# Memory keys and values at plain float32 from the loaded weights, the norm weights in the memory

## Chip, cores and metric

The kernel runs on one core of one Trainium2 chip. The metric is the device time of one execution in microseconds (us), here the median of three runs. All data are float32. The kernel hands float32 data to TensorE under two types, `F32R` (less precise) and plain `F32`.

## The reference, cut to what matters

Two layers of an encoder on 256 tokens of width 1024. The even layer mixes by RWKV-7 and a state-space model (S5), the odd one by differential attention; either is followed by cross-attention to a memory of 256 rows, then by a feed-forward part (dense in the first layer, the two best of eight experts in the second). What the change touches is the left side of the cross-attention, which depends on the memory alone:

```python
def rms_norm(x, gain):
    y = x * rsqrt(mean(x * x, axis=-1) + 1e-6)
    return y * gain

def memory_cross_attention(h, mem_n, w_q, w_kv, q_gain, k_gain, w_o):
    q = rms_norm((h @ w_q).reshape(b, t, 4, 256), q_gain)
    k, v = split(mem_n @ w_kv, 2)            # w_kv: 1024 x 2048
    k = rms_norm(k.reshape(b, m, 4, 256), k_gain)
    p = softmax(q . k * 256 ** -0.5)
    return (p @ v) @ w_o

# in layer l: mem_n = rms_norm(mem, norm_mem[l])
```

The factor of a memory row, the rsqrt, is the same in both layers; the norm weights `norm_mem[l]` and the weights `w_kv[l]` are a layer's own.

## The kernel before, in words

Every large product is made to a higher precision than one `F32R` matmul gives. A float32 operand is split in two: ScalarE writes its high half as `F32R` (`AF.Copy`), VectorE subtracts that from the operand and writes the low half. `mm3` (line 188) then adds three `F32R` matmuls to one PSUM tile: high by high, high by low, low by high (lines 190, 191, 192). `mm` (line 194, its matmul in line 195) issues one matmul of whatever type its operands have; with `F32` operands it is a plain float32 one, which the trace shows as two records. The split weights of the large products come from `chunks` (line 164), which loads, splits and yields them.

The first third of a millisecond holds the RWKV and S5 mixing of the first layer. It is a chain of small products and elementwise work that goes back and forth between TensorE, VectorE, ScalarE and GpSimd. The keys and values of both layers, which depend on the memory alone, are computed beside it as filler:

- `memory_norm` (line 462) loads the memory in two blocks of 128 rows, multiplies each by its rsqrt factor, and has `transpose_split` (line 203) transpose it, four pieces of 128 columns to a PSUM tile, and write it split, as `mth` and `mtl` (128 x 8 x 256 each).
- `fchunks` (line 437) loads the weights of 512 output columns, two blocks of 128 rows at a time, into `fraw` (pool `frw`, two buffers) from SP's queue. Each block is split: ScalarE multiplies it by the norm weights of its rows and writes the high half `fwh` (line 450), VectorE does the same product, subtracts and writes the low half `fwl` (line 453). Pool `fwp` has three buffers of each.
- `memory_kv` (line 477) does this for the two layers: for each of four groups of 512 output columns and each of eight blocks of rows it issues two `mm3`, one per block of memory rows, into the two PSUM tiles `pf`; then it scales, transposes and stores keys, or copies and stores values. That makes 2 x 4 x 8 x 2 = 128 memory products.

`memory_kv` is a generator: after every product it yields an estimate of TensorE's time in us, `0.65`. `pipeline` (in the kernel's first part) deals out such steps. It walks through the steps of the chain with estimated costs and waits, and puts steps of the filler between them: the memory products, then the rest of the S5 scan, the S5 gate (`s5_gate`) and the first half of the out projection (`hy_first`). The filler gets half a us per us of the chain (`FILL_B`), 16 us ahead of it (`FILL_C`), and every estimated wait. The order in which the code is issued in this way is a priority; in this part of the kernel the framework's scheduler makes each engine's own order from it, and from there every engine runs its queue in order. Norm and first filler steps are issued with a lowered priority (`LPM`, `LPF`).

After this part the kernel frees its pools, and the second half of the out projection, the first cross-attention, the dense feed-forward part, the second layer's attention and the experts follow. The order of TensorE is written out by hand there. The keys and values come back from DRAM for either cross-attention.

Of the kernel before, what the change touches and what calls it, by code (L numbers as in the profile page):

```python
# [8 lines left out]
F32 = mybir.dt.float32  # L9
F32R = mybir.dt.float32r  # L10
I32 = mybir.dt.int32
AF = mybir.ActivationFunctionType
# [111 lines left out]
def kernel(ctx: ExitStack, tc: tile.TileContext, a: dict, out: bass.AP, dbg=None):  # L124
# [10 lines left out]
    def scoped(cx, name, bufs, **kw):  # L135
        return cx.enter_context(tc.tile_pool(name=name, bufs=bufs, reuse_waits="tile", **kw))
# [87 lines left out]
    xtp1 = pool("xtp1", 1, reuse_waits="tile", side="right")  # L224
    cright = ExitStack()
    fkp = scoped(cright, "fkp", 1, side="right")
    frw = scoped(cright, "frw", 2, side="right")
    fwp = scoped(cright, "fwp", 3, side="right")
    fs2 = scoped(cright, "fs2", 2, side="right")
    smf = scoped(cright, "smf", 2, side="right")  # L230
    cx = ExitStack()
# [202 lines left out]

    low_priority(lambda: [behind(S5BT, lambda: s5_table(m)) for m in range(2)], LPT)

    def fchunks(src, nk=8, gain=None):
        for r in range(0, nk, 2):
            raw = frw.tile([128, 1024], F32, name="fraw", tag="fraw")
            nc.sync.dma_start(raw, src[:, r * 512:(r + 2) * 512])  # L440
            for j in range(2):
                wh = fwp.tile([128, 512], F32R, name="fwh", tag="fwh")
                wl = fwp.tile([128, 512], F32R, name="fwl", tag="fwl")
                rv = raw[:, j * 512:(j + 1) * 512]
                if gain is None:
                    nc.scalar.activation(wh, rv, AF.Copy)
                    nc.vector.tensor_tensor(wl, rv, wh, op=ALU.subtract)
                else:
                    g = col(gain, r + j)
                    nc.scalar.activation(wh, rv, AF.Copy, scale=g)  # L450
                    e_ = nc.gpsimd if FG[W["fg"] % len(FG)] == "g" else nc.vector
                    W["fg"] += 1
                    e_.scalar_tensor_tensor(wl, rv, g, wh, op0=ALU.mult, op1=ALU.subtract)  # L453
                yield r + j, wh, wl


    kdr = [tc.dram_tile([4, 128, 512], F32, name=f"kdr{l}") for l in range(2)]
    vdr = [tc.dram_tile([4, 128, 512], F32, name=f"vdr{l}") for l in range(2)]
    mth = fkp.tile([128, 8, T], F32R, name="mth")
    mtl = fkp.tile([128, 8, T], F32R, name="mtl")  # L460

    def memory_norm():
        for b in range(2):
            mem = sp.tile([128, D], F32, name="mem", tag="mem")
            nc.sync.dma_start(mem, a["mem"][b * 128:(b + 1) * 128, :])
            ss = smf.tile([128, 1], F32, name="ss", tag="ss")
            for i in range(2):
                kx = fs2.tile([128, 512], F32, name="kx", tag="kx")
                s1 = ss if i == 0 else smf.tile([128, 1], F32, name="ssb", tag="ssb")
                nc.scalar.activation(kx, mem[:, i * 512:(i + 1) * 512], AF.Square, accum_out=s1)  # L470
            nc.gpsimd.tensor_tensor(ss, ss, s1, op=ALU.add)
            rs = smf.tile([128, 1], F32, name="rs", tag="rs")
            rsqrt_small(rs, ss, 1, 1.0 / D, EPS, smf)
            nc.vector.tensor_scalar(mem, mem, rs, None, op0=ALU.mult)
            transpose_split(mem, mth, mtl, 0, b, ps_fl, "fl")

    def memory_kv(l):
        gg = const.tile([128, 2], F32, name=f"gg{l}")
# [2 lines left out]
        nc.gpsimd.tensor_tensor(gg, cols[:, lo:hi], cols[:, lo2:hi2], op=ALU.mult)  # L481
        for n in range(4):
            p = [ps_fl.tile([128, 512], F32, name="pf", tag="fl") for b in range(2)]
            for k, wh, wl in fchunks(a["wkv"][4 * l + n], 8, f"gm{l}"):
                for b in range(2):
                    t = slice(b * 128, (b + 1) * 128)
                    mm3(p[b], (mth[:, k, t], mtl[:, k, t]), (wh, wl), k == 0, k == 7)
                    yield 0.65
            for b in range(2):
                kx = fs2.tile([128, 512], F32, name="kx", tag="kx")  # L490
                if n >= 2:
# [1716 lines left out]
```

## Time and profile before

| what | us |
|---|---|
| median of three runs | 1673.35 |
| lowest and highest run | 1672.85, 1676.12 |
| the profiled execution | 1672.61 |
| its span, first to last instruction | 1670.8 |
| TensorE busy | 1619.4 (97%) |
| VectorE busy | 639.9 (38%) |
| ScalarE busy | 476.1 (28%) |
| GpSimd busy | 198.5 (12%) |

The shares are means over parts of the run that have different limits, so the rows below are given by stretch. In the profile PE is TensorE's matmuls and PEld its weight loads, DVE is VectorE, ACT ScalarE, POOL GpSimd and SP the engine that issues most DMAs. Matmuls overlap, and their ends are modelled: a TensorE that is busy all the time may still have room. How fast matmuls follow one another is read from their starts in the timeline. In the chain of waits every piece is work that was waited for, or the instruction before it on the same engine; "issue" is time in which nothing that the profile shows was waited for.

### The profile page before, as it was taken

How to read it: one execution, taken by the hardware profiler on the slowest of the kernel's cores; microseconds unless marked ns; L12 is line 12 of the kernel's file. 1: busy time of each engine (PE TensorE's matmuls, PEld its weight loads, DVE VectorE, ACT ScalarE, POOL GpSimd, SP SyncE). 2: the span in 40 equal slices, each digit the busy share in tenths (PEclk: the TensorE clock that was granted, in tenths of full speed). 3: DMA queues.
4: the chain of work that ended last, by engine and by line, in shares of the span. 5: the costliest groups of instructions: out<-in, count | busy, mean ns of one | idle time of the engine just before them, and what ended most of it. 6: DMA issues, size and time to landing. Idle time of an engine off the chain costs nothing.

```text
span 1670.8 us, 34308 instructions
## 1 busy us (share of the span) xinstructions
PE 1619.4 (97%) x14882; PEld 982.9 (59%) x14882; DVE 639.9 (38%) x1065; ACT 476.1 (28%) x852; POOL 198.5 (12%) x230
## 2 busy tenths in 40 slices
PE   6999999999999999999999999999999999999997
PEld 5877657899999988998334333343333433333432
DVE  7778987676555567764100011100101001010011
ACT  6466434555544456653101000010000100010000
POOL 6334473111000031110000000000000000000000
PEclk9999979999999999998999999999999999999999
DMA  6423323664555543646699889999999999999995
GB/s 227 152 89 127 109 71 115 222 255 152 186 193 180 195 156 116 239 150 239 252 387 383 333 356 407 415 418 419 419 418 418 419 419 419 418 419 387 372 419 218
DMA packets 74462, 471.48 MB, mean 282 GB/s; under 512 B 8600, under 2 KB 10008, under 8 KB 22464
## 3 DMA queue, kind: packets, MB, share of 16 engines
q1 hardware_dynamic: 73024, 465.02, 71.5%
q0 software_dynamic: 1280, 4.20, 0.7%
q8 instruction: 118, 1.93, 0.5%
q14 instruction: 40, 0.33, 0.1%
HBM read 463.94 MB, written 5.24 MB: 281 GB/s over the span
## 4 chain that ended last, share of the span: by engine, by line
PE 86%; DVE 8%; ACT 2%; POOL 2%; issue 2%; DMA 0%; SPq 0%; DVEq 0%; POOLq 0%; ACTq 0%
PE pgu L195 31%; PE pd L195 16%; PE pm L190 5%; PE pm L192 5%; PE pm L191 5%; PE pgu L190 2%; PE pgu L192 2%; PE pgu L191 2%; PE pm L195 2%; PE pgt L195 1%; PE pf L190 1%; PE pf L191 1%; PE pf L192 1%; PE po L195 1%; DVE zz L569 1%
## 5 line engine op out<-in xcount | busy, mean ns | idle before, releaser
L195 PE MATMUL pgu<-raw,gx 128*32 128x512 f32 (+1 forms) x5376 | 515.8, 542 | 0.0
L195 PEld LDWEIGHTS pgu<-raw,gx 128*32 128x32 f32 x5376 | 171.9, 110 | 319.8 <-issue 287.2
L195 PE MATMUL pd<-raw,th 128*32 128x512 f32 x2352 | 266.4, 607 | 0.4 <-DVE th L1896 0.4
L184 DVE TENSOR_TENSOR wl<-raw,wh 128x1024 fp32r<-128x1024 f32 (+1 forms) x159 | 195.0, 1238 | 103.2 <-ACT wh L178 102.8
L178 ACT ACTIVATE wh<-raw 128x1024 fp32r<-128x1024 f32 (+1 forms) x160 | 165.5, 1047 | 146.8 <-PE pgu L191 67.7
L1882 DVE SCALAR_TENSOR_TENSOR actA<-pgu,gs,actA 128x512 f32<-128x512 f32 (+1 forms) x32 | 21.9, 684 | 468.0 <-PE pgu L195 282.7
L195 PEld LDWEIGHTS pd<-raw,th 128*32 128x32 f32 x2352 | 75.5, 112 | 175.2 <-issue 171.7
L190 PE MATMUL pm<-xh,wh 128*128 128x256 f32 (+1 forms) x552 | 161.6, 296 | 14.4 <-ACT wh L178 12.4
L192 PE MATMUL pm<-xh,wl 128*128 128x256 f32 (+1 forms) x552 | 158.0, 290 | 4.9 <-DVE wl L184 4.9
L191 PE MATMUL pm<-xl,wh 128*128 128x256 f32 (+1 forms) x552 | 159.0, 289 | 2.2 <-DVE xl L1096 2.2
L1878 ACT ACTIVATE actA<-pgu,gs 128x512 f32<-128x512 f32 (+1 forms) x32 | 20.3, 634 | 448.5 <-PE pgu L195 433.5
L190 PEld LDWEIGHTS pm<-xh,wh 128*128 128x128 f32 (+1 forms) x552 | 107.6, 196 | 17.5 <-ACT wh L178 12.9
L192 PEld LDWEIGHTS pm<-xh,wl 128*128 128x128 f32 (+1 forms) x552 | 106.7, 195 | 7.1 <-DVE wl L184 6.4
L191 PEld LDWEIGHTS pm<-xl,wh 128*128 128x128 f32 (+1 forms) x552 | 107.8, 195 | 3.7 <-DVE xl L1096 2.6
L1896 DVE COPY th<-ptA 128x384 f32<-128x384 f32 (+3 forms) x32 | 14.9, 464 | 245.0 <-PE ptA L1895 245.0
L191 PE MATMUL pgu<-xl,wh 128*128 128x256 f32 x352 | 98.6, 280 | 0.0
L190 PE MATMUL pgu<-xh,wh 128*128 128x256 f32 x352 | 98.5, 280 | 0.0
L192 PE MATMUL pgu<-xh,wl 128*128 128x256 f32 x352 | 98.5, 280 | 0.0
L192 PEld LDWEIGHTS pgu<-xh,wl 128*128 128x128 f32 x352 | 66.2, 188 | 0.0
L191 PEld LDWEIGHTS pgu<-xl,wh 128*128 128x128 f32 x352 | 66.2, 188 | 0.0
L190 PEld LDWEIGHTS pgu<-xh,wh 128*128 128x128 f32 x352 | 66.1, 188 | 0.0
L453 DVE SCALAR_TENSOR_TENSOR fwl<-fraw,cols,fwh 128x512 fp32r<-128x512 f32 x64 | 56.9, 896 | 11.4 <-ACT fwh L450 11.3
(477 smaller groups left out, 2138.9 us busy)
## 6 DMA issues: line engine op xcount, KB each, us to landing
raw<-mg SPq DMA_DIRECT2D x112, 1024.0 KB, 15.5
raw<-mu SPq DMA_DIRECT2D x112, 1024.0 KB, 15.3
raw<-md SPq DMA_DIRECT2D x112, 1024.0 KB, 14.9
raw<-wgu SPq DMA_DIRECT2D x22, 1024.0 KB, 4.9
fraw<-wkv SPq DMA_DIRECT2D x32, 512.0 KB, 4.1
raw<-wqkv SPq DMA_DIRECT2D x12, 1024.0 KB, 4.9
raw<-wdn SPq DMA_DIRECT2D x11, 1024.0 KB, 4.9
raw<-hy SPq DMA_DIRECT2D x16, 512.0 KB, 3.8
```

The costliest lines, as they stand in the source:

```text
L178: W["act"].append(nc.scalar.activation(wh, rv, AF.Copy).ins)
L184: W["dve"].append(e_.tensor_tensor(wl[:, c_], rv[:, c_], wh[:, c_], op=ALU.subtract).ins)
L190: nc.tensor.matmul(out, lhsT=lt[0], rhs=r[0], start=start, stop=False, **kw)
L191: nc.tensor.matmul(out, lhsT=lt[0], rhs=r[1], start=False, stop=False, **kw)
L192: nc.tensor.matmul(out, lhsT=lt[1], rhs=r[0], start=False, stop=stop, **kw)
L195: nc.tensor.matmul(out, lhsT=lt, rhs=r, start=start, stop=stop, **kw)
L453: e_.scalar_tensor_tensor(wl, rv, g, wh, op0=ALU.mult, op1=ALU.subtract)
L569: nc.vector.tensor_tensor_scan(z[:, ri], rho[:, j:j + 1].to_broadcast([128, T]), xc[:, ri], 0.0, op0=ALU.mult, op1=ALU.add)
L1878: nc.scalar.activation(actA, p[0], AF.Silu, scale=gs[:, 0, 1:2])
L1882: nc.vector.scalar_tensor_tensor(actA, p[1], gs[:, 0, 1:2], actA, op0=ALU.mult, op1=ALU.mult)
L1896: nc.vector.tensor_copy(th[:, 0], ptA[:, :, 0:c])
```

## The change

The split of the memory weights goes, and with it the pool `fwp` and the two instructions per block of 128 rows. The matmul reads the block where it was loaded; `frw` has four buffers instead of two. A memory product is one plain float32 matmul (`mm`) instead of the three of `mm3`. The norm weights, which had been multiplied into the weights, are multiplied into the memory: instead of one split memory there are two float32 copies, `mts[0]` and `mts[1]`, one for each layer. They are written from the same transposed PSUM tiles, `mts[0]` by ScalarE and `mts[1]` by VectorE, 128 columns at a time since each has its own column of weights. The estimated cost of a product is 0.86 instead of 0.65.

```diff
@@ -224,8 +224,7 @@
     xtp1 = pool("xtp1", 1, reuse_waits="tile", side="right")
     cright = ExitStack()
     fkp = scoped(cright, "fkp", 1, side="right")
-    frw = scoped(cright, "frw", 2, side="right")
-    fwp = scoped(cright, "fwp", 3, side="right")
+    frw = scoped(cright, "frw", 4, side="right")
     fs2 = scoped(cright, "fs2", 2, side="right")
     smf = scoped(cright, "smf", 2, side="right")
     cx = ExitStack()
@@ -434,30 +433,17 @@
 
     low_priority(lambda: [behind(S5BT, lambda: s5_table(m)) for m in range(2)], LPT)
 
-    def fchunks(src, nk=8, gain=None):
+    def fchunks(src, nk=8):
         for r in range(0, nk, 2):
             raw = frw.tile([128, 1024], F32, name="fraw", tag="fraw")
             nc.sync.dma_start(raw, src[:, r * 512:(r + 2) * 512])
             for j in range(2):
-                wh = fwp.tile([128, 512], F32R, name="fwh", tag="fwh")
-                wl = fwp.tile([128, 512], F32R, name="fwl", tag="fwl")
-                rv = raw[:, j * 512:(j + 1) * 512]
-                if gain is None:
-                    nc.scalar.activation(wh, rv, AF.Copy)
-                    nc.vector.tensor_tensor(wl, rv, wh, op=ALU.subtract)
-                else:
-                    g = col(gain, r + j)
-                    nc.scalar.activation(wh, rv, AF.Copy, scale=g)
-                    e_ = nc.gpsimd if FG[W["fg"] % len(FG)] == "g" else nc.vector
-                    W["fg"] += 1
-                    e_.scalar_tensor_tensor(wl, rv, g, wh, op0=ALU.mult, op1=ALU.subtract)
-                yield r + j, wh, wl
+                yield r + j, raw[:, j * 512:(j + 1) * 512]
 
 
     kdr = [tc.dram_tile([4, 128, 512], F32, name=f"kdr{l}") for l in range(2)]
     vdr = [tc.dram_tile([4, 128, 512], F32, name=f"vdr{l}") for l in range(2)]
-    mth = fkp.tile([128, 8, T], F32R, name="mth")
-    mtl = fkp.tile([128, 8, T], F32R, name="mtl")
+    mts = [fkp.tile([128, 8, T], F32, name=f"mt{l}") for l in range(2)]
 
     def memory_norm():
         for b in range(2):
@@ -472,7 +458,14 @@
             rs = smf.tile([128, 1], F32, name="rs", tag="rs")
             rsqrt_small(rs, ss, 1, 1.0 / D, EPS, smf)
             nc.vector.tensor_scalar(mem, mem, rs, None, op0=ALU.mult)
-            transpose_split(mem, mth, mtl, 0, b, ps_fl, "fl")
+            for g in range(0, 8, 4):
+                pt = ps_fl.tile([128, 4, 128], F32, name="pt", tag="fl")
+                for c in range(4):
+                    nc.tensor.transpose(pt[:, c], mem[:, (g + c) * 128:(g + c + 1) * 128], ident)
+                for c in range(4):
+                    t = slice(b * 128, (b + 1) * 128)
+                    nc.scalar.activation(mts[0][:, g + c, t], pt[:, c], AF.Copy, scale=col("gm0", g + c))
+                    nc.vector.tensor_scalar(mts[1][:, g + c, t], pt[:, c], col("gm1", g + c), None, op0=ALU.mult)
 
     def memory_kv(l):
         gg = const.tile([128, 2], F32, name=f"gg{l}")
@@ -481,11 +474,10 @@
         nc.gpsimd.tensor_tensor(gg, cols[:, lo:hi], cols[:, lo2:hi2], op=ALU.mult)
         for n in range(4):
             p = [ps_fl.tile([128, 512], F32, name="pf", tag="fl") for b in range(2)]
-            for k, wh, wl in fchunks(a["wkv"][4 * l + n], 8, f"gm{l}"):
+            for k, w in fchunks(a["wkv"][4 * l + n]):
                 for b in range(2):
-                    t = slice(b * 128, (b + 1) * 128)
-                    mm3(p[b], (mth[:, k, t], mtl[:, k, t]), (wh, wl), k == 0, k == 7)
-                    yield 0.65
+                    mm(p[b], mts[l][:, k, b * 128:(b + 1) * 128], w, k == 0, k == 7)
+                    yield 0.86
             for b in range(2):
                 kx = fs2.tile([128, 512], F32, name="kx", tag="kx")
                 if n >= 2:
```

## Rows read from the trace of the kernel before

**Rows 1.** Page part 2, one digit a slice: busy tenths of the DMA engines.

```profile
DMA  6423323664555543646699889999999999999995
```

**Rows 2.** Stretches of the whole run; columns: length, then busy us (count) by engine, clock, DMA.

```profile
342.00:790.00 448.00, 441.98 (x3431) 425.33 (x3429) 278.90 (x438) 227.15 (x384) 51.25 (x44) 0.99 0.53 186
790.00:1670.80 880.80, 864.80 (x8240) 311.83 (x8240) 93.39 (x198) 70.25 (x147) 0.00 (x0) 0.98 0.94 385
```

**Rows 3.** The same columns for stretches of the first 342 us.

```profile
60.00:100.00 40.00, 40.00 (x248) 33.54 (x247) 22.01 (x33) 23.55 (x44) 5.95 (x8) 1.00 0.47 152
100.00:140.00 40.00, 36.40 (x217) 29.97 (x216) 33.04 (x44) 22.68 (x51) 15.06 (x13) 0.91 0.32 106
140.00:200.00 60.00, 58.62 (x986) 38.86 (x987) 56.02 (x94) 28.53 (x47) 29.51 (x31) 1.00 0.38 120
200.00:260.00 60.00, 54.26 (x917) 35.01 (x917) 52.70 (x81) 25.44 (x48) 39.44 (x43) 0.82 0.20 63
260.00:312.00 52.00, 52.00 (x360) 41.15 (x359) 33.74 (x61) 24.71 (x48) 10.80 (x18) 0.98 0.42 142
312.00:342.00 30.00, 30.00 (x239) 29.26 (x239) 22.83 (x29) 18.19 (x27) 5.79 (x6) 1.00 0.80 302
```

**Rows 4.** Chain that ended last, by line: stretches 60-100, 100-140, 140-200, 200-260, 260-312.

```profile
by line: PE pm L195 17.5%; PE pm L191 14.8%; PE pm L192 14.5%; PE pm L190 14.2%; PE pf L190 11.0%; PE pf L192 10.4%; PE pf L191 10.3%; PE pk L195 4.2%; PE ptf L508 2.9%; PE pr L659 0.5%
by line: DVE fwl L453 13.8%; DVE ka L727 8.3%; PE pm L192 7.0%; PE pm L190 5.0%; PE pm L191 5.0%; DVE cs L709 4.7%; DVE v L638 4.7%; issue 4.2%; DVE zz L569 4.2%; DVE z L626 3.5%; DVE zz L562 3.2%; DVE bt L723 3.1%; DVE xc L561 2.9%; DVE wl
by line: DVE fwl L453 13.0%; DVE zz L569 11.7%; issue 10.8%; PE pm L195 5.7%; DVE wl L184 5.7%; DVE zz L562 5.1%; DVE tbl L413 4.4%; DVE xc L561 4.1%; DVE tbl L414 4.1%; DVE xc L571 3.8%; PE pf L190 3.6%; DVE zz L574 3.3%; DVE a L801 3.3%; 
by line: issue 13.5%; DVE zz L569 12.2%; DVE fwl L453 8.2%; PE py L195 7.8%; POOL xc L576 5.8%; POOL xc L564 5.4%; PE pm L195 5.2%; DVE xc L571 4.9%; POOL xc L575 4.8%; POOL xc L563 4.3%; DVE zz L562 4.2%; DVE xc L561 3.3%; DVE zz L574 2.2%
by line: PE pm L195 24.3%; PE pf L191 16.1%; PE pf L190 15.7%; PE pf L192 14.9%; PE po L195 13.0%; PE pm L190 4.0%; PE pm L191 4.0%; PE pm L192 3.6%; PE py L195 3.2%; PE ptf L508 2.3%
```

**Rows 5.** Line 453 (the low halves) alone, on VectorE, in three of those stretches.

```profile
100.00:140.00 40.00, 7.90 (x8) 0.91 0.32 106
140.00:200.00 60.00, 15.47 (x16) 1.00 0.38 120
200.00:260.00 60.00, 11.72 (x13) 0.82 0.20 63
```

**Rows 6.** Instructions of tiles pf, fwh, fwl: ns min/median/max, first and last start.

```profile
L190 PE MATMUL pf<-fwh,mth x128: 387/397/775, 60.0 to 316.0; 128*128 128x512 f32 x128
L450 ACT ACTIVATE fwh<-fraw,cols x64: 703/722/740, 24.7 to 311.6; 128x512 fp32r<-128x512 f32 x64
L453 DVE SCALAR_TENSOR_TENSOR fwl<-fraw,cols,fwh x64: 720/748/2864, 28.0 to 312.3; 128x512 fp32r<-128x512 f32 x64
```

**Rows 7.** Timeline of TensorE: start, us; memory products, then a plain float32 product and after.

```profile
60.00 0.40 PE L190 MATMUL pf<-fwh,mth 128*128 128x512 f32 x1
60.69 0.39 PE L190 MATMUL pf<-fwh,mth 128*128 128x512 f32 x1
92.61 0.59 PE L195 MATMUL pm<-gup,zr 128*128 128x512 f32 x1
93.04 1.64 PE L195 MATMUL pm<-gup,zr 128*128 128x512 f32 x3
96.72 0.48 PE L195 MATMUL pm<-zr,wlr 64*128 64x256 f32 x1
```

**Rows 8.** VectorE on PSUM tiles: the present memory split, and a 128-column scaled copy.

```profile
L212 DVE TENSOR_TENSOR mtl<-pt,mth x4: 672/676/678, 38.7 to 57.2; 128x512 fp32r<-128x512 f32 x4
L896 DVE SCALAR_TENSOR_TENSOR S<-pm,dec,hcst x12: 343/344/351, 264.9 to 295.6; 128x128 f32<-128x128 f32 x12
```

**Rows 9.** Timeline around 117 us: GpSimd's product and a low half on VectorE.

```profile
115.59 3.88 POOL L738 TENSOR_TENSOR rkp<-r,k 128x1024 f32<-128x1024 f32 x1 [3.54 <-DVE r L638]
117.16 2.86 DVE L453 SCALAR_TENSOR_TENSOR fwl<-fraw,cols,fwh 128x512 fp32r<-128x512 f32 x1
```

**Rows 10.** Page part 6, the memory weights: KB each, median us from issue to landing.

```profile
fraw<-wkv SPq DMA_DIRECT2D x32, 512.0 KB, 4.1
```

## The prediction

> **What bounds the kernel now.** I read the run from its end. From 790 us on the DMA engines are at nine tenths or more in nearly every slice [rows 1], and from 342 to 790 us TensorE is busy for 442 of 448 us [rows 2]. The change touches nothing in either part, and the last memory product starts at 316 us [rows 6]. So what counts is when the first 342 us end: I carry a shift there through to the end one for one.
>
> Within the first 342 us there are two kinds of stretch [rows 3]. From 60 to 100 and from 260 to 342 us TensorE is busy the whole time. Between them, from 100 to 260 us, VectorE is busy for 33.0 + 56.0 + 52.7 = 141.8 of 160 us. TensorE shows 36.4 + 58.6 + 54.3 = 149.3 us there, but its matmuls overlap and their modelled ends run on while the next has begun, so this is no full load. The chain of waits says which of the two is late [rows 4]. In 60 to 100 and 260 to 312 us it names TensorE alone, and the memory products (tile pf, lines 190 to 192) hold 31.7% and 46.7% of it. In the middle the largest or third largest entry is line 453, the low half of the memory weights on VectorE: 13.8%, 13.0% and 8.2%. The change takes that entry away and makes the pf entries dearer; the forecast is the balance of the two.
>
> **Removed.** 64 high halves on ScalarE at a median 722 ns and 64 low halves on VectorE at a median 748 ns [rows 6]. The first are 46 us of an engine that is busy less than 60% in each stretch [rows 3], and the chain does not name it: I cost them at nothing, as VectorE and TensorE cover them; were ScalarE the bound, they would be worth up to 46 us. Of the second, 7.9 + 15.5 + 11.7 = 35.1 us lie between 100 and 260 us [rows 5]. Their chain shares give 13.8% of 40, 13.0% of 60 and 8.2% of 60 us: 5.5 + 7.8 + 4.9 = 18.2 us. Nothing (something else is late at once) and 35.1 us are the ends; I take 18.2, as the chain leaves out the instructions beside which something else was as late. What is late next: the additions of the state-space scan on GpSimd, in 200 to 260 us 5.8 + 5.4 + 4.8 + 4.3 = 20.3% of the chain, and TensorE itself. Outside 100 to 260 us the low halves stand beside a full TensorE and give nothing.
>
> A word on their length. One low half took 2.86 us instead of 0.75, and it lay beside a GpSimd product of 3.88 us that ended just before it did [rows 9]. [...] Without the 2.1 us of this one wait the chain's 18.2 us would be 16.1.
>
> **Added on TensorE.** A memory product is three F32R matmuls now, and starts 60.69 - 60.00 = 0.69 us after the one before it [rows 7]. After the change it is one plain float32 matmul of the same 128x512 shape. The trace has such a matmul, the gate's product: its two records start at 92.61 and 93.04 us, 0.43 us apart, so two of them are 0.86 us; the eight records from 92.61 to 96.72 us, which change the rows they use from pair to pair, give 4.11 / 4 = 1.03 us for one [rows 7]. The memory products keep their rows, so I take 0.86: 0.17 us more each. There are 128 (each of the three lines has 128 records, [rows 6]), so 21.8 us of TensorE in all, 43.5 by the other end. I leave the dearer end out of the range but for its edge, since the products of today pay for such changes too.
>
> On the path stand those in the stretches where TensorE is the chain: 31.7% of 40 = 12.7 us and 46.7% of 52 = 24.3 us [rows 4], and from 312 to the last of them at 316 us [rows 6] about 4.9 us. Dearer by 0.17 / 0.69 = 25%, that is 3.1 + 6.0 + 1.2 = 10.3 us. In 100 to 260 us only line 190's 3.6% of 60 = 2.2 us is listed: 0.5 us more. The other products of that stretch lie beside VectorE's work, which hides them; if that cover is gone they cost the rest, 21.8 - 10.8 = 11.0 us.
>
> [...]
>
> **Moved.** The norm weights go into the memory: for each of four PSUM tiles one split pair becomes four ScalarE and four VectorE copies of 128x128. VectorE had 0.68 us a tile and gets four of at most 0.34 [rows 8], 1.4 us. The last split starts at 57.2 us and the first product at 60.0, so the last tile's surplus of 0.7 us may reach the path; I charge 0.6. The bounds are 0 and 4 x 0.7 = 2.8 us.
>
> The weights' DMAs (32 of 512 KB, 4.1 us to landing, [rows 10]) wait in SP's queue for a buffer. Today VectorE gives it back after the low half; after, TensorE does after the product. Four buffers hold eight blocks of 128 rows, 16 products or 13.7 us, three times the landing time. Behind a waiting one stand the RWKV weights on the same queue, and TensorE, whose own queue is in order, would stand still if one came late. I cost it at nothing; that is the last rival.
>
> **The sum.** -18.2 + 10.3 + 0.5 + 0.6 = -6.8 us. The profiled execution took 1672.6 us, 0.7 below the median of 1673.35; 1672.6 - 6.8 + 0.7 gives 1666.5 us. About 0.2%, 3.3 us, is what a measurement of this kernel can tell from no change.
>
> **Rivals.** *TensorE becomes the bound of the middle stretch (slower).* For it: TensorE shows work for 149.3 of 160 us there, and the fill is dealt out by cost, so dearer products leave more of themselves to the end, where TensorE is full. Against it: VectorE's gaps are as small, and the chain names VectorE. Price: 21.8 + 0.6 us, less half of TensorE's 10.7 us without work there, as far as those were waits for low halves: +17.1, or 1690 us. It decides once the middle stretch gets shorter by less than 10.3 + 0.5 + 0.6 = 11.4 us.
>
> *Another wait takes the place (no change).* GpSimd's additions follow VectorE's scan and are followed by its next one [rows 4]; if half of the 18.2 us passes to them, -9.1 + 11.4 = +2.3, or 1675.6 us.
>
> *The whole load counts (faster still).* If VectorE's queue, always full, is the only bound, 35.1 us come off: -35.1 + 11.4 = -23.7, or 1649.6 us. [...] Against it: 18.2 us of 35.1 is what the chain found.
>
> *The products do not run as written, since their weights come late.* If each of the 32 blocks came late by a tenth of its landing time, that would be 13 us: -6.8 + 13, or 1680 us. The 13.7 us of cover speak against it.
>
> **How the numbers follow.** The forecast has 0.38, TensorE as the bound 0.30, another wait 0.17, the whole load 0.12, late weights 0.03. Faster: 0.38 + 0.12 = 0.50. Same: 0.17. Slower: 0.30 + 0.03 = 0.33. The range reaches from the whole load's 1649 to the 1690 of TensorE as the bound; the forecast's own is 1658 to 1671 (VectorE's gain between 14 and 27 us).
>
> **What would show it.** Right: the out projection's last products end near 335 us instead of 342; VectorE loses some 35 us of work between 100 and 260 us and is no longer the chain's main engine there; a memory product is two records 0.43 us apart. Wrong: the middle stretch as long as before with TensorE in the chain, or more than the present few memory products left after the last RWKV block. The prediction fails if the compiler's order puts the dearer fill behind the chain instead of into its gaps.

## The result, and the profile after

The changed kernel takes 1701.7 us (median of four runs, 1698.6 to 1704.4), the kernel before 1673.9 in the same comparison: a ratio of 1.0172, 95% interval 1.0149 to 1.0195. It is slower by about 28 us, where 7 us faster was forecast, and it lies outside the range. In the two profiled executions the span grew by 31.8 us, from 1670.8 to 1702.6. One of the four runs of e10 below was a slow one (2382.9 us at a granted clock of 0.65), and the medians and ratios leave it out.

First what came as forecast. The page's busy times, and the memory product's own rows (form: ns min/median/max, first and last start):

```profile
PE 1638.5 (96%) x14754; PEld 963.0 (57%) x14754; DVE 588.0 (35%) x1013; ACT 433.0 (25%) x798; POOL 189.6 (11%) x230
...
L195 PE MATMUL pf<-fraw,mt x256: 590/592/1222, 67.8 to 345.4; 128*128 128x512 f32 x128
```

VectorE shows 588.0 us instead of 639.9, and a product is two records, 256 for 128. What a product costs is read from runs of them in the chain of waits of 100 to 140 us (start, length, what; x16 are eight products):

```profile
by line: PE pf L195 52.0%; PE pm L195 13.2%; PE pm L192 5.3%; PE pm L190 5.2%; POOL rsk L201 4.9%; PE pm L191 4.7%; PE pb L195 4.7%; PE ptf L500 4.6%; issue 2.2%; POOL kdr L507 1.6%; ACT kx L504 1.3%; ACT kx L496 1.2%; POOL rsq L200 0.5%
...
103.26 6.87 PE pf L195 x16
...
111.19 7.06 PE pf L195 x16
...
128.25 6.87 PE pf L195 x16
```

6.87 / 8 = 0.86 us, the price taken from [rows 7]. But these three lines also hold the surprise. In the kernel before the products of this stretch lay a few at a time between steps of the chain, and VectorE's low half led the list [rows 4]. Now runs of eight stand in TensorE's queue, and they lead the list: 52.0% of 40 us.

The same stretches as in [rows 3] (length, busy us and count by engine, clock, DMA):

```profile
60.00:100.00 40.00, 39.77 (x227) 29.35 (x226) 18.52 (x30) 17.28 (x35) 5.21 (x6) 1.00 0.45 145
100.00:140.00 40.00, 38.69 (x175) 23.62 (x174) 17.05 (x22) 17.08 (x42) 17.79 (x13) 1.00 0.25 86
140.00:200.00 60.00, 55.90 (x538) 34.56 (x538) 44.54 (x79) 18.18 (x33) 24.55 (x29) 0.83 0.33 111
200.00:260.00 60.00, 46.62 (x1242) 27.33 (x1238) 38.01 (x72) 10.29 (x18) 28.12 (x36) 0.77 0.11 38
260.00:312.00 52.00, 51.44 (x317) 31.75 (x316) 23.25 (x45) 15.16 (x41) 15.36 (x21) 0.97 0.34 115
312.00:342.00 30.00, 30.00 (x125) 16.06 (x124) 7.81 (x14) 6.67 (x12) 2.16 (x8) 1.00 0.40 134
```

From 140 to 260 us TensorE is busy for 102.5 us instead of 112.9, and the granted clock is 0.83 and 0.77 where it was 1.00 and 0.82. That the fill is missing there shows in tile pf alone, in 168 to 236 us, first after, then before (up to 260 us this tile is written by memory products alone; columns as above, without GpSimd):

```profile
168.00:236.00 68.00, 2.84 (x6) 1.06 (x6) 0.00 (x0) 0.00 (x0) 0.67 0.06 21
```

```profile
168.00:236.00 68.00, 27.77 (x93) 16.37 (x93) 0.00 (x0) 4.53 (x14) 0.89 0.31 98
```

Six records of 256 are three products; 93 of 384 were 31. They were made earlier, where they held up the chain, or are left for later. The chain of 200 to 260 and of 312 to 370 us after:

```profile
by line: issue 16.0%; DVE zz L561 13.2%; POOL xc L555 8.4%; POOL xc L556 8.0%; POOL xc L568 6.2%; DVE xc L563 5.8%; PE pm L195 5.1%; POOL zz L566 4.4%; PE py L195 4.2%; DVE zz L566 3.0%; POOL xc L567 3.0%; DVE xc L553 2.2%; DVE zz L554 2.0%
```

```profile
by line: PE pf L195 48.0%; PE pf L191 13.2%; PE pf L190 13.1%; PE pf L192 13.1%; PE po L195 4.5%; PE pm L195 3.6%; PE pt L208 1.5%; PE pm L190 1.4%; PE pm L192 1.2%; PE pm L191 1.0%
...
338.90 7.07 PE pf L195 x16
```

In the middle it now waits for the state-space scan on VectorE and GpSimd (lines 553 to 568, "issue" beside them) with little from TensorE; from 312 us on, where memory products were nearly done before [rows 6], they are 48.0% of the chain. The last starts at 345.4 us instead of 316.9.

By landmarks of the chain: VectorE's last instruction on tile v, behind the last RWKV projection, came at 147.0 instead of 136.2 us (+10.8; 43 memory products had started by then, 32 before). The inversion's first product (pm from aa and a constant) came at 192.0 instead of 160.7 us: here the whole delay, 31.3 us, is already made, with 61 memory products started instead of 45. The inversion gives 15.4 us of it back. Its last product (pm from qq and vt) came at 266.5 instead of 250.6 us, with 12 memory products started since its first instead of 41, and without the low halves on VectorE. From there to the last addition of the out projection it took 13.7 us more: 55 memory products are left for it instead of 42, and 55 x 0.86 is 18.3 us more of TensorE than 42 x 0.69. At the experts' first product the delay is 31.5 us, and nothing after 342 us gives it back.

The granted clock has a part in this. In the first 400 us the clock granted to TensorE is down to half (0.50, as in 225 to 240 us before) for 61.4 us after, for 41.0 us before. What such time costs can be estimated from the four runs of one kernel, e9 below: two, at a mean granted clock of 0.979 and 0.978, took 1695.7 and 1694.8 us, the other two, at 0.973 and 0.974, 1703.8 and 1703.3 us. That is 8.3 us for 0.005 of the clock, which over 1700 us is 17 us more at half the clock: about half a us for one. The fastest and the slowest run of e3, 1681.8 us at 0.975 and 1691.2 at 0.967, give a third. By this estimate the 20.4 us more are worth some 7 to 10 of the 28 us.

### The profile page after: what moved, and what is told of

It is laid out like the page before. It is cut to its first block, busy times and chain, and to the rows that moved or that the text cites. A ratio compares the mean times of both kernels' runs of the same rounds, so it can differ in the third digit from the quotient of the medians.

```text
span 1702.6 us, 33892 instructions
## 1 busy us (share of the span) xinstructions
PE 1638.5 (96%) x14754; PEld 963.0 (57%) x14754; DVE 588.0 (35%) x1013; ACT 433.0 (25%) x798; POOL 189.6 (11%) x230
## 4 chain that ended last, share of the span: by engine, by line
PE 88%; DVE 5%; POOL 3%; ACT 3%; issue 1%; DMA 0%; SPq 0%; POOLq 0%; DVEq 0%; ACTq 0%
PE pgu L195 30%; PE pd L195 15%; PE pf L195 6%; PE pm L190 5%; PE pm L192 5%; PE pm L191 5%; PE pgu L190 2%; PE pgu L191 2%; PE pgu L192 2%; PE pm L195 2%; PE pgt L195 1%; PE po L195 1%; PE psc L195 1%; PE ptA L1887 1%; DVE zz L561 1%
## 5 line engine op out<-in xcount | busy, mean ns | idle before, releaser
L195 PE MATMUL pf<-fraw,mt 128*128 128x512 f32 x256 | 119.2, 609 | 0.0
L195 PEld LDWEIGHTS pf<-fraw,mt 128*128 128x128 f32 x256 | 46.7, 192 | 52.4 <-issue 50.7
L192 PEld LDWEIGHTS pgu<-xh,wl 128*128 128x128 f32 x352 | 66.2, 188 | 0.0
L191 PEld LDWEIGHTS pgu<-xl,wh 128*128 128x128 f32 x352 | 66.2, 188 | 0.0
## 6 DMA issues: line engine op xcount, KB each, us to landing
raw<-mu SPq DMA_DIRECT2D x112, 1024.0 KB, 15.4
```

Source lines behind the costliest of these rows:

```text
L191: nc.tensor.matmul(out, lhsT=lt[0], rhs=r[1], start=False, stop=False, **kw)
L192: nc.tensor.matmul(out, lhsT=lt[1], rhs=r[0], start=False, stop=stop, **kw)
L195: nc.tensor.matmul(out, lhsT=lt, rhs=r, start=start, stop=stop, **kw)
```

## The experiments

At this point two theories stood. *Order:* the low halves on VectorE had been what held the filler back; without them, and with the larger count of 0.86 us a product, products bunch up ahead of the chain and are missing beside it. *Price:* TensorE is the bound, and the 21.8 us of dearer products are the loss, whatever the order. The table has all runs; ratios are to the kernel before in the same comparison. "inv" is the start of the last product of w and aa, the last product but one on the inversion's path (the expectations call it the last small inversion matmul), "out" of the last product of the RWKV output (tile po), "add" of the out projection's last addition, "exp" of the experts' first product; "products" counts the memory products started by inv and by out; "low" is the time, in the first 400 us, in which TensorE was granted half its clock (0.50). The columns behind the ratio are of the profiled execution.

| kernel | us | ratio, 95% interval | products | inv | out | add | exp | low |
|---|---|---|---|---|---|---|---|---|
| before | 1673.9 | | 84, 121 | 244.4 | 308.7 | 341.3 | 793.7 | 41.0 |
| after | 1701.7 | 1.0172, 1.0149 to 1.0195 | 67, 120 | 251.1 | 337.2 | 370.8 | 825.2 | 61.4 |
| e1 | 1694.9 | 1.0144, 1.0115 to 1.0174 | 84, 128 | 252.0 | 333.5 | 362.8 | 813.4 | 37.5 |
| e2 | 1693.6 | 1.0128, 1.0100 to 1.0155 | 106, 128 | 267.6 | 334.7 | 363.8 | 815.3 | 41.0 |
| e3 | 1685.7 | 1.0072, 1.0044 to 1.0099 | 67, 96 | 237.2 | 298.2 | 354.7 | 811.3 | 61.4 |
| e4 | 1715.9 | 1.0293, 1.0234 to 1.0352 | 84, 128 | 280.4 | 353.3 | 385.0 | 836.8 | 122.9 |
| e5 | 1671.6 | 1.0003, 0.9990 to 1.0016 | 80, 123 | 234.8 | 300.3 | 338.9 | 793.8 | 27.3 |
| e6 | 1709.2 | 1.0230, 1.0213 to 1.0247 | 84, 121 | 267.9 | 336.7 | 376.6 | 830.0 | 30.7 |
| e7 | 1701.3 | 1.0179, 1.0162 to 1.0196 | 128, 128 | 289.7 | 341.5 | 372.4 | 823.5 | 58.0 |
| e8 | 1682.6 | 1.0059, 1.0040 to 1.0077 | 80, 124 | 246.5 | 321.3 | 354.5 | 805.5 | 37.5 |
| e9 | 1699.5 | 1.0165, 1.0129 to 1.0202 | 84, 128 | 261.6 | 339.9 | 368.2 | 820.2 | 44.4 |
| e10 | 1709.6 | 1.0211, 1.0146 to 1.0276 | 84, 124 | 270.3 | 344.1 | 377.2 | 831.0 | 64.9 |
| e11 | 1696.8 | 1.0139, 1.0113 to 1.0165 | 80, 120 | 251.8 | 325.4 | 365.6 | 819.1 | 34.1 |
| e12 | 1702.5 | 1.0180, 1.0162 to 1.0198 | 96, 128 | 267.5 | 338.2 | 371.7 | 823.9 | 61.4 |

Gains and losses below are differences of these ratios times 1673 us; "either way" gives the half width of a 95% interval.

### The order: the count, the pace, and the reverse edits

Four runs change where the products stand, and nothing of their work.

e1, the changed kernel with the old count:

```diff
-                    yield 0.86
+                    yield 0.65
```

> The changed kernel with one number put back: a memory product counts as 0.65 instead of 0.86 when the filler is dealt out. All instructions are those of the changed kernel, in another order on TensorE. Order theory: the changed kernel lost 20 us because some 23 products left the middle stretch, where the chain waits, for the end, where TensorE is full; with 0.65 as many products lie ahead of the last small inversion matmul as before (84 of 128 instead of 67), so about 12 of the 28 us come back: 1688 to 1692 us. Price theory: the dearer products cost what they cost wherever they lie, since TensorE is full throughout: 1700 to 1704 us.

e2, the changed kernel with the filler dealt out at twice the pace:

```diff
-FILL_B = 0.5
+FILL_B = 1.0
```

> The changed kernel with one other number changed: the filler gets 1.0 us instead of 0.5 per us of the chain, so that 106 of the 128 products lie ahead of the last small inversion matmul and all of them ahead of the RWKV output. Order theory: more comes back than with the 0.65, since the granted clock in the middle stays up and nothing of the products is left for the end: 1680 to 1690 us. Price theory: 1700 to 1704 us.

e3, the kernel before with the new count:

```diff
-                    yield 0.65
+                    yield 0.86
```

> The kernel before with one number changed: a memory product counts as 0.86 instead of 0.65. Splits, matmuls and price stay. Order theory: some 17 products leave the middle and 26 come after the RWKV output, where TensorE is full: 12 to 18 us slower than before, 1686 to 1692 us, with no dearer product in it. Price theory: no change, 1672 to 1676 us.

e3 makes the kernel before slower by 12 us with no change in any instruction: the chain comes earlier (inv 237.2 instead of 244.4), but 32 products are left after out instead of 7, and TensorE makes them when everything else waits for it (the trace is of the slowest of its four runs, 1691.2 us). e1 and e2 give back 5 and 7 us of the 28, each 6 either way, which is hardly clear of noise and less than the order theory had on record. The trace shows the order changed, since no product is left after out in either, and in e1 TensorE's time at half the clock falls from 61.4 to 37.5 us. So the order counts in the kernel before (e3); in the changed kernel these two edits leave most of the loss.

e7 asks whether earlier is better for the kernel before as well:

```diff
-FILL_B = 0.5
+FILL_B = 1.0
```

> The kernel before with 1.0 instead of 0.5 us of filler per us of the chain, nothing else: all 128 products lie ahead of the RWKV output in TensorE's order. Order theory: the place of the filler decides, and the middle stretch has room for more of it: 1664 to 1671 us, faster than before. If TensorE is full in the middle too, the chain only gets later: 1672 to 1680 us.

It is worse by 30 us, more than either theory allowed. All 128 products stand ahead of inv, which comes 45 us late, and afterwards TensorE lacks work, here in 342 to 370 us, with the clock down:

```profile
342.00:370.00 28.00, 18.05 (x117) 16.75 (x117) 19.93 (x30) 12.53 (x20) 3.65 (x4) 0.71 0.99 388
```

(28.00 of 28 us at 1.00 in the kernel before.) Too early costs as well as too late: 30 us here, 12 in e3.

### VectorE's share alone

e5 leaves out 63 of VectorE's 64 low halves in the kernel before, and nothing else:

```diff
-                wl = fwp.tile([128, 512], F32R, name="fwl", tag="fwl")
+                wl = W.get("cl")
...
-                    e_.scalar_tensor_tensor(wl, rv, g, wh, op0=ALU.mult, op1=ALU.subtract)
+                    if wl is None:
+                        wl = W["cl"] = fkp.tile([128, 512], F32R, name="fwl")
+                        e_.scalar_tensor_tensor(wl, rv, g, wh, op0=ALU.mult, op1=ALU.subtract)
```

> The kernel before without 63 of its 64 low halves: one low half is made from the first block and read by every product, so the products are not the reference's. ScalarE's high halves, the three F32R matmuls of 512 columns and 0.65 stay, and TensorE's order is nearly that of before (80 of 128 products ahead of the last small inversion matmul, 84 before). It measures what the low halves cost on VectorE, alone. If VectorE's share of the chain was worth the 18 us of the prediction: 1652 to 1658 us. If its queue was full without being the limit: 1668 to 1674 us.

1671.6 us, ratio 1.0003: the term of -18.2 us, the whole gain of the forecast, is worth nothing by itself (2 us either way). The chain did get earlier, by 9.6 us at inv and 8.4 at out; the last memory product starts 11.9 us earlier. The lead is lost behind them: 6.3 us are left at the last transposition of the RWKV output, 0.6 at the last product of the out projection. 300 to 320 us in e5 and before:

```profile
300.00:320.00 20.00, 13.18 (x88) 11.83 (x87) 11.04 (x18) 6.77 (x12) 3.54 (x9) 0.83 0.68 268
```

```profile
300.00:320.00 20.00, 20.00 (x137) 16.61 (x137) 13.52 (x21) 9.53 (x15) 3.48 (x9) 1.00 0.32 98
```

TensorE has 13.2 us of work in 20 where it was full, at a clock of 0.83. What it waits for is in the chain of 304 to 318 us (line numbers two higher than in the kernel before):

```profile
305.27 0.62 ACT sqo L928
...
306.38 0.73 ACT t L959 x2
307.11 0.95 ACT wh L178
...
308.08 1.23 DVE wl L184
...
309.82 0.75 DVE uT L960 x2
310.58 0.60 DVE os L936
311.18 0.61 DVE uT L961
...
313.11 1.15 DVE xl L966
...
314.30 0.58 PE pf L191
```

These are the norm of the RWKV output (os), the split of the next weights (wh, wl) and the S5 gate (t, uT, xl), on ScalarE and VectorE, one after the other. Before, TensorE was full in this time, with memory products up to 317 us; here the last starts at 305.0 us, and the elementwise work stands bare. A shift of the first 300 us is therefore not carried "through to the end one for one": only the part that the last fill can cover is.

### TensorE's share alone

e6 gives each memory product of the kernel before a fourth F32R matmul, the low half of the memory by the low half of the weights: 0.23 us more each, 29.4 us in all.

```diff
-                    mm3(p[b], (mth[:, k, t], mtl[:, k, t]), (wh, wl), k == 0, k == 7)
+                    mm3(p[b], (mth[:, k, t], mtl[:, k, t]), (wh, wl), k == 0, False)
+                    mm(p[b], mtl[:, k, t], wl, False, k == 7)
```

> The kernel before with a fourth F32R matmul in every memory product, low by low, which the reference does not need: 128 x 0.23 = 29.4 us more of TensorE; the splits, the count of 0.65 and nearly the order stay (84 products ahead of the last small inversion matmul). It measures what more TensorE work per product costs. If the products of the middle stretch hide it, as the prediction had it (10.8 of 21.8 us on the path): +15 us, 1685 to 1690 us. If TensorE has no room there either: +27 to +32, 1699 to 1705 us.

+38 us (3 either way) for 29.4, 1.3 times the price and more than either theory had, at an order close to the old one (84 and 121 products by inv and out, as before) and with less time at half the clock (30.7 us, 41.0 before). So with the low halves in place the forecast's step "beside VectorE's work, which hides them" is wrong, although VectorE is as busy as ever in 200 to 260 us and TensorE is not full:

```profile
200.00:260.00 60.00, 52.80 (x1085) 34.01 (x1074) 55.47 (x93) 21.33 (x39) 32.17 (x38) 0.94 0.20 63
```

inv comes 23.5 us later. A reading that fits, argued and not shown: a longer product that stands in TensorE's queue between two steps of the chain delays the second, and with it VectorE's next instruction, so that the busier engine does not cover the other.

e4 was to give the changed kernel the old price: for each product one F32 column of the real one, and two F32R matmuls of constant data (tile mcc, filled once) in the place of the rest.

```diff
-                    mm(p[b], mts[l][:, k, b * 128:(b + 1) * 128], w, k == 0, k == 7)
-                    yield 0.86
+                    t = slice(b * 128, (b + 1) * 128)
+                    mm(p[b][:, 0:1], mts[l][:, k, t], w[:, 0:1], k == 0, False, skip_group_check=True)
+                    mm(p[b], mcc[:, 0:128], mcc, k == 0, False, skip_group_check=True)
+                    mm(p[b], mcc[:, 128:256], mcc, False, k == 7, skip_group_check=True)
+                    yield 0.65
```

> The changed kernel with products that cost TensorE about what they did before: two F32R matmuls of 512 columns on a constant tile and one plain float32 matmul of a single column that reads the loaded block, and 0.65 as their count. The real product is left out, so the output is not the reference's. No split is left on VectorE and ScalarE, TensorE has no more work than before. It measures what the freed VectorE is worth by itself. If the 18 us that the prediction took from the chain are right: 1654 to 1660 us. If VectorE's queue was full without being the limit (the chain's own round trips and GpSimd are): 1668 to 1674 us.

It tells nothing of the price, since TensorE got half the clock for 122.9 of its first 400 us (41.0 before):

```profile
140.00:200.00 60.00, 57.70 (x577) 43.58 (x576) 29.64 (x51) 20.50 (x39) 18.07 (x24) 0.66 0.35 116
```

TensorE is shown as busy for 57.7 of 60 us, and the granted clock is 0.66. What brought the clock down, the one-column matmuls, the constant data or something else, was not shown.

### Both together

If VectorE's low halves are worth nothing at the old price, they may be worth something at the new one, since the end then has fill to spare. e11 is e6 without 63 of the low halves; e8 and e10 are the changed kernel with and without VectorE's work. e8 lets ScalarE copy each block into a tile of its own, as the high half was copied before, with two load buffers again and the count of 0.65; e10 adds VectorE's low half as work that nobody reads.

e8, against the changed kernel:

```diff
-    frw = scoped(cright, "frw", 4, side="right")
+    frw = scoped(cright, "frw", 2, side="right")
+    fwp = scoped(cright, "fwp", 3, side="right")
...
-                yield r + j, raw[:, j * 512:(j + 1) * 512]
+                wc = fwp.tile([128, 512], F32, name="fwc", tag="fwc")
+                nc.scalar.activation(wc, raw[:, j * 512:(j + 1) * 512], AF.Copy)
+                yield r + j, wc
...
-                    yield 0.86
+                    yield 0.65
```

> The changed kernel with 0.65 and with the loaded block copied by ScalarE into a buffer of three before the product reads it (two raw buffers, as before). Price as changed, no VectorE work, but the products come to TensorE one or two at a time and not in runs of eight (61 runs instead of 32). If the runs of eight held up the chain: 1680 to 1688 us, clearly below the 1694.9 of the run with 0.65 alone. If only the dearer product counts: 1691 to 1697 us.

e10, against e8:

```diff
                 nc.scalar.activation(wc, raw[:, j * 512:(j + 1) * 512], AF.Copy)
+                wl = fwp.tile([128, 512], F32R, name="fwl", tag="fwl")
+                nc.vector.scalar_tensor_tensor(wl, raw[:, j * 512:(j + 1) * 512], col("gm0", r + j), wc, op0=ALU.mult, op1=ALU.subtract)
                 yield r + j, wc
```

> e8_scalar_copy (the changed kernel, count 0.65, block copied by ScalarE) with VectorE's 64 low halves put back as work that nobody reads. TensorE's memory products stay one plain float32 product each. Theory 'VectorE's freed time is worth nothing, also with dearer products' (as e5_one_low showed for the cheaper ones): 1680 to 1686 us. Rival 'VectorE's freed time paid for half of the 21.8 us that the products became dearer; without it the whole price shows': 1692 to 1698 us, with the inversion's last product some 8 us later than in e8.

e11, against e6, the edit of e5 in short:

```diff
-                wl = fwp.tile([128, 512], F32R, name="fwl", tag="fwl")
+                wl = W.get("cl")
...
+                    if wl is None:
+                        wl = W["cl"] = fkp.tile([128, 512], F32R, name="fwl")
```

> e6_fourth_matmul (the kernel before with a fourth F32R matmul in each memory product, 0.23 us more each, 29.4 us of TensorE in all) with a single low half of the weights kept and VectorE's other 63 left out; the low half that is multiplied is therefore the first block's for all blocks. Theory 'TensorE alone sets the stage's end': 1705 to 1711 us, as e6's 1709. Rival 'freed VectorE is worth something as soon as TensorE is dearer': 1690 to 1700 us, the chain of the inversion at least 10 us earlier than in e6 and the gain kept to the experts' first product.

e11 is 15 us faster than e6 (5 either way), e8 25 us faster than e10 (11 either way; e10 is slower than either theory had). So the rival that freed VectorE pays once TensorE is dearer holds in both pairs, and "worth nothing" holds only at the old price. The first pair is the clean one. In the second e10 has 27.4 us more at half the clock (64.9 instead of 37.5), which at half a us each may be up to 14 of the 25, and a load buffer is held until VectorE has read it (SP's queue waits 214.8 us in all for that in 60 to 350 us): in 140 to 200 us of e10 a late load is 5.7% of the chain. Read the other way, the runs price the products without the low halves: from e5 to e11 the fourth matmul costs 23 us (5 either way) and not 38, and from e5 to e8 the plain float32 product with the scaled memory costs 9 us (4 either way) and not the 35 from the kernel before to e10. The two prices do not add; each depends on whether the other is paid. In e11 the lead over e6 is 16.1 us at inv, 11.3 at out, 11.0 at the last addition and 10.9 at the experts: it is kept, where e5's was lost. The chain of 200 to 260 us by line in e8, then in e10:

```profile
by line: PE pf L195 34.7%; PE pm L195 12.9%; PE pbu L195 8.8%; PE py L195 7.6%; DVE zz L564 5.4%; DVE tbl L413 4.0%; issue 3.5%; DVE tbl L414 2.6%; POOL xc L558 2.5%; DVE xc L566 2.2%; POOL xc L559 2.2%; DVE zz L557 2.1%; POOL zz L569 2.1%;
```

```profile
by line: DVE zz L566 12.2%; DVE fwl L445 11.8%; issue 9.6%; PE pf L195 7.7%; DVE zz L559 5.2%; DVE xc L568 5.0%; DVE xc L558 4.1%; DVE tbl L413 3.8%; DVE zz L571 3.2%; POOL xc L572 2.8%; DVE tbl L414 2.6%; DVE qq L820 2.5%; POOL xc L560 2.4
```

In e8 TensorE leads, in e10 VectorE's scan and the low halves (11.8%), with the same products. In e8 TensorE has next to no time without work from 140 to 260 us:

```profile
140.00:200.00 60.00, 60.00 (x751) 34.32 (x750) 32.16 (x59) 26.81 (x54) 23.03 (x30) 0.89 0.32 104
200.00:260.00 60.00, 59.54 (x1090) 29.87 (x1089) 49.28 (x84) 28.05 (x55) 40.15 (x49) 0.97 0.25 83
```

against 58.62 and 54.26 us before [rows 3]. It is the best form of the change found here, and still 10 us slower than the kernel before.

### What made e8 better than e1

e8 differs from e1 in ScalarE's copy and in the number of buffers, and is faster by 14 us (6 either way). In its queue no run of products is longer than six. e9 has the changed kernel's products straight from the loaded block, with two buffers instead of four, which also breaks most runs of eight:

```diff
-    frw = scoped(cright, "frw", 4, side="right")
+    frw = scoped(cright, "frw", 2, side="right")
...
-                    yield 0.86
+                    yield 0.65
```

> The changed kernel with the count of 0.65 (as e1_yield065) and two weight buffers instead of four, no copy on ScalarE. In TensorE's queue no run of memory products stands that is longer than four but for two, where e1 has runs of eight. Theory 'runs of eight come from the four buffers': as good as e8_scalar_copy, 1680 to 1686 us. Rival 'the copy on ScalarE made the difference, because a copied block frees the DMA's buffer early': like e1, 1692 to 1698 us, with TensorE waiting for weights in the timeline. In between: both have a part.

1699.5 us, no better than e1: doing away with most runs of eight is not enough by itself. e9 and e8 differ in the copy alone, and that is 18 us (7 either way). Both have 56 memory products started when the inversion's first product of w and aa starts (193.3 us in e8, 193.4 in e9), and both lay the same 30 between there and the inversion's last product (qq and vt), which comes at 256.5 us in e8 and at 266.9 in e9. These two stretches, e8 and then e9:

```profile
193.30:256.50 63.20, 62.74 (x1285) 31.68 (x1284) 53.48 (x92) 27.29 (x53) 40.97 (x49) 0.97 0.22 71
```

```profile
193.40:266.90 73.50, 68.29 (x1293) 34.97 (x1292) 54.73 (x95) 16.68 (x36) 43.57 (x54) 0.91 0.23 74
```

So e9 has no less fill there, but it takes 10 us longer over it: TensorE shows 5.2 us without work instead of 0.5, and the clock is 0.91 instead of 0.97. The fill lies differently. Up to 248 us e8 has one or two products between two steps, while e9 has three, four and three together at 213, 221 and 229 us. A block that ScalarE copies gives its load buffer back after the copy, and one that TensorE reads is held until TensorE's queue has come past its products: SP's queue waits for the copy in e8 (194.9 us in all in 60 to 350 us) and for the products in e9 (202.2 us). But TensorE waits for no load in e9, which the rival on record had expected. That the held buffers are why the products come bunched, and the bunching why they cost more, is argued, not shown.

e12 is e8 with a count of 0.55, to see whether more could be put into the gaps:

```diff
-                    yield 0.65
+                    yield 0.55
```

> e8_scalar_copy with the count lowered from 0.65 to 0.55, so that in TensorE's queue 96 instead of 80 memory products stand ahead of the inversion's last one, and all 128 ahead of the last product of the RWKV output (e8: 124). Theory 'TensorE is now the bound of the whole stage, so the order can give no more': 1680 to 1686 us, as e8's 1682.6, or worse as in e7_before_fillb1, where all products came too early. Rival 'e8 still leaves products to the end that would fit into earlier gaps': 1674 to 1679 us.

1702.5 us, 20 us worse than e8 (4 either way). inv comes 21 us later, with 96 products started by then instead of 80, and TensorE has 23.9 us more at half the clock (61.4 instead of 37.5). As in e7, products that come too early delay the chain.

## Why the prediction was wrong

Two steps failed. The forecast added the gain of the low halves, -18.2 us, to a price of 11.4 us for the products and the norm, as if each stood by itself; the low halves alone are worth 0 (e5), and both changes together, in e8, come to +10 us where the forecast had -6.8. And it costed what else the change takes away or moves at nothing, ScalarE's copies and the fill's order; from e8 to the changed kernel these are another +19 us.

One way from the kernel before to the one after, in us against before: e10 has the dearer products and the scaled memory, with VectorE's work still there (+35); e8 takes that work away (-25); e1 takes away ScalarE's copy and gives four load buffers for two (+14); the count of 0.86 makes it the changed kernel (+5, within noise). The sum, +29, is the measured difference by construction, and what a step is worth depends on the way: with the low halves taken away first it is 0 (e5) and then +9 to e8. The steps of the forecast one by one:

**The price of a product, 0.86 us, was right.** The three runs of eight above give 0.86 to 0.88 us for one, not the dearer end of 1.03, and 0.86 - 0.69 is 0.17.

**What the products cost on the path hangs on VectorE's load.** Of 21.8 us the forecast charged 10.8 and let VectorE's work hide the rest. Beside the low halves that failed: e6 shows 1.3 times the full price, e10 about 35 us (11 either way) for 21.8. Without them the size was fair, 9 us from e5 to e8 against 11.4 with the norm, but for the opposite reason: VectorE's work does not hide the products, its absence makes room for them. The chain of waits names one releaser per wait; that VectorE came last in 100 to 260 us did not mean that TensorE had slack there, since the chain runs through both.

**The -18.2 us for the low halves were no constant.** With the old products they are worth 0 (e5), with dearer ones about 15 (e11), and up to 25 (e10) with a part of that due to the clock. The size was fair and the condition was missing: in e5 the lead of the chain was lost where no fill was left to cover the elementwise work behind it, and the forecast carried it to the end "one for one".

**That nothing else moves was wrong.** The high halves on ScalarE were costed at nothing, "as VectorE and TensorE cover them". As a load they were nothing, but the copy is worth 14 us (6 either way, from e8 to e1, with the buffers) or 18 (7 either way, from e8 to e9), in part through the clock; the rest of the reason stays open. The forecast named a failure of the order in its last sentence, "the dearer fill behind the chain instead of into its gaps", and gave it no price. That was half of it: the inversion lost 29 products, of which 16 moved ahead of it and 13 behind. The sign of being wrong that came true was the other one, a middle stretch as long as before: from tile v to the inversion's last product it took 119.5 us instead of 114.4. The rival "TensorE becomes the bound" had the right sign and, by e8, the right mechanism. Its 1690 us lacked the copies and the order.

**The norm's copies were mis-sized**, and what that did to the end was not isolated. The copies of the memory (ns min/median/max, first and last start):

```profile
L467 ACT ACTIVATE mt<-pt,cols x16: 341/359/369, 38.6 to 64.1; 128x128 f32<-128x128 f32 x16
L468 DVE TENSOR_SCALAR mt<-pt,cols x16: 321/340/351, 39.7 to 65.4; 128x128 f32<-128x128 f32 x16
```

Each is as long as taken from [rows 8], but they are not done back to back: ScalarE's waited 7.7 us in all for VectorE's and VectorE's 0.7 us for ScalarE's, and the first memory product starts at 67.8 instead of 60.0 us, where 2.8 us was the bound. TensorE is full there with other work, but in the first 60 us it shows 37.6 us of work instead of 41.3, so up to 3.7 us may have been lost. e8, with the same copies (first product at 66.2), reaches the end of tile v at 132.0, before the 136.2 of the kernel before, though with fewer products started (24 instead of 32).

**Late weights** were no cause. The waits of SP's queue after, and the weights' DMAs (KB each, median us):

```profile
SPq L439 <- PE pf L195: 177.1, 26, 39.7
```

```profile
fraw<-wkv SPq DMA_DIRECT2D x32, 512.0 KB, 5.0
```

The queue waits for TensorE's products to give buffers back (177.1 us in 26 waits, the longest 39.7), as forecast; a load takes 5.0 instead of 4.1 us [rows 10], and TensorE waits 0.2 us in all for a block to land.

**The long low half** is gone, but GpSimd's product beside it got longer. Before, that low half took 2.1 us more than the others beside GpSimd's product of 3.88 us [rows 9]. After, VectorE and GpSimd around that product:

```profile
127.02 1.21 DVE L715 TENSOR_TENSOR bt<-bt,kk 128x1024 f32<-128x1024 f32 x1
128.16 1.21 DVE L722 TENSOR_TENSOR kt<-k,en 128x1024 f32<-128x1024 f32 x1
129.29 1.21 DVE L728 TENSOR_TENSOR ar<-r,ec 128x1024 f32<-128x1024 f32 x1
130.43 2.35 DVE L184 TENSOR_TENSOR wl<-raw,wh 128x1024 fp32r<-128x1024 f32 x2
```

```profile
127.18 7.80 POOL L730 TENSOR_TENSOR rkp<-r,k 128x1024 f32<-128x1024 f32 x1 [0.30 <-DVE r L630]
```

Now GpSimd's product takes 7.80 us beside five VectorE instructions of 1.2 us in a row, none of which is lengthened, and ends 2.2 us after the last of them. It is about as long in e5 (7.73 us) and e9 (7.74), where this product is 19.4% of the chain of 100 to 140 us, and shorter in e8 (4.36). Why VectorE's instruction is the longer one in one kernel and GpSimd's in another was not shown.

One reading was slightly off: ScalarE is busy for 18.19 of 30 us in 312 to 342 us [rows 3], 61% and not less than 60%; nothing hangs on it.

Left open: why the copy on ScalarE is worth 14 to 18 us, how much of each step is the clock, and whether a queue written out by hand would bring the changed kernel to the time before; no version here beats it.

## What to carry to other kernels

Where a chain goes back and forth between two engines and a filler shares both, gains on one engine and costs on the other do not add: here the same dearer filler cost 38 us beside the other engine's work and 23 without it, and taking that work away gave 0 or 15 us. So price such changes together, and test each with and without the other. Count a lead of the chain as a gain only if something covers what stands behind it. Instructions that look free, like copies on an idle engine, can still be worth something (14 to 18 us here); before such a change, alter only the filler's count or pace once, and see what the order by itself is worth (12 us in e3 and 30 in e7). The share of the chain that an entry holds says who came last, not how far behind the next one is.

## What the runs showed of the hardware

A GpSimd product of 128x1024 took 3.88, 4.36, 6.63 or 7.80 us in four of the kernels (before, e8, e10, after), and in each it ended 2.2 us after the last of the VectorE instructions of 128x1024 that took their 1.2 us beside it. And TensorE was granted a mean clock of 0.66 while shown as busy for 57.7 of 60 us: in 140 to 200 us of e4, where the memory products were one-column matmuls and matmuls of constant data.
